# A chunked recurrence whose key products take all 128 rows of the array, with zeros where the solved values will stand, and one late gate instead of two

## The chip, the cores and the metric

The kernel runs on one core of one Trainium2 chip. The metric is device time in microseconds (us), start to end of one execution. The engines are named as in the profile: PE (TensorE, matrix products; PEld is its weight load), DVE (VectorE), ACT (ScalarE), POOL (GpSimd) and SP, whose queue issues nearly all transfers. Each engine takes its instructions in the order in which the program holds them; a semaphore holds an instruction back until what it reads is there.

## What is computed

One layer of a decoder trunk in float32: 512 tokens, width 1024. A combined projection feeds a dilated attention, a recurrent mixer (RWKV-7) of 16 heads and two gates; their gated sum goes through an output product, then a gated feed-forward part follows. The change lies in the recurrent mixer:

```python
def step(state, inp):
    r_t, w_t, k_t, v_t, aa_t, bb_t = inp
    sa = jnp.einsum('bhvk,bhk->bhv', state, aa_t)
    state = state * w_t[:, :, None, :] + sa[..., None] * bb_t[:, :, None, :] + v_t[..., None] * k_t[:, :, None, :]
    return state, jnp.einsum('bhvk,bhk->bhv', state, r_t)
...
_, y = lax.scan(step, state0, (tm(r_h), tm(w_h), tm(k_h), tm(v_h), tm(-kk), tm(kk * a_h)))
...
g_att, g_rwkv = jnp.split(jax.nn.sigmoid(gate_in + b_gate[l]), N_BRANCHES, axis=-1)
x = x + gt1 * ((g_att * y_att + g_rwkv * y_rwkv) @ w_o[l])
```

Every `sa` depends on the state after the token before, so the heads' recurrences are sequential in the tokens.

## The kernel before

Exact products of float32 matrices are made of three products each, of a rounded high part and the rest (`whi`, `wlo`, `hhi`, `hlo`): eight blocks of the contraction make 24 products of 128x128 by 128x512 on PE for one block of 128 output columns. Such a block is called a body.

**The recurrence** goes through the 512 tokens in 8 chunks of 64. The 16 heads form four groups of four; a group consists of two pairs `i` = 0, 1 of two heads `h` each. For a group, `pair()` makes r, k, v, decays and the Gram matrices `gt` of the chunks (on PE with the names `pg`, `pt`, `pn`); `inverse()`, and `inverse16()` for the last group, invert the triangular part of all chunks on DVE, with a few small products at the end (`pe`); `chain()` then runs the chunks one behind the other. A chunk `c` consists of:

- `state` (planned as `xy`): into the accumulator `xy` go the products of the carried state with the row matrix (`xy<-mbd,ar`, from the second chunk on) and the products of the Gram matrix with the values (`xy<-uv,gt`); these last are the keys' products of the title;
- `state_out`: the products of the carried state for the output, `xo<-mbd,ar`;
- `xs` on ACT copies `xy` out, `solve` multiplies it by the inverse (`u<-xs,gt`), and `solved` on ACT writes the result into `uv`;
- `update` (`u<-uv,bkt`) and `carry` on DVE make the new state `mbd`; `mp` on POOL multiplies the old state by its decay beforehand;
- `outs` (`xo<-uv,gt`) adds the output's share of the chunk; `norm` scales the outputs by two chunks.

The tile `uv` holds, for two chunks at once, values and solved quantities side by side: of its 128 rows, 64 hold the values of a chunk and the other 64 are what `solved` fills; which half is which changes with the chunk and with `i` (`R[i]`, `X[i]`). `values` (`u<-cen,v`) and `value` on ACT fill the first half for both chunks. There are two buffers of it. The keys' product reads the 64 rows of values alone, `outs` reads all 128.

**The order** is made when the program is built. `Plan` simulates the engines with a cost for each task that is written beside it, with priorities and with counted buffers; the sequence in which its tasks start becomes each engine's order. The keys' product is line 1804; the planned costs of `state` and `state_out` are in lines 1850 and 1851. Tasks of the recurrence have the first priority; bodies of projections, gates and later products have the last on PE and take what is left, in the order of their numbers.

**The gates** are 16 bodies (`pg`). An early gate is computed before its consumers' buffers exist, stored to memory (`gate_d`) and loaded again. The attention output's products (`pa`) need the attention halves `a`, which `att_parts` loads (`raw<-att_d`), casts on ACT and subtracts on DVE (line 2052). That may start only when all work that uses an earlier memory pool is done, all early gates among it. A late gate (`self.late`, line 1079) is computed after that point, straight into its place. The last products are `pr`, the recurrent mixer's output weights.

The weights come through two buffers, `raw`, of 1024 elements per partition; they are shared with the attention halves' load.

Of the kernel before, what the change touches and what calls it, by code (L numbers as in the profile page):

```python
# [10 lines left out]
F32 = mybir.dt.float32  # L11
# [7 lines left out]
P = 128  # L19
S = 512  # L20
D = 1024
KD = D // P
# [95 lines left out]
C_, E_, W_, V_, I_, M_, S_, U_ = 0.0, 1.0, 2.0, 200.0, 200.15, 220.0, 1.0, 10.0  # L118
# [10 lines left out]
class Layer:  # L129
# [911 lines left out]
    def rwkv(self, tail):  # L1041

        nc, tc, pl = self.nc, self.tc, self.pl
        self.cw, self.cps, self.ip, self.pps = [Late() for _ in range(4)]
        self.gps = [Late(), Late()]
        es, pre, even = self.rw_ctx, self.pre_ctx, ExitStack()

        def open_():
            self.att_ctx.close()
            pool = lambda st, room, name, bufs=1, **kw: setattr(  # L1050
                room, "pool", st.enter_context(tc.tile_pool(name=name, bufs=bufs, reuse_waits="tile", **kw)))
            pool(es, self.cw, "cw", 2)
            pool(es, self.gps[1], "gp1", 4)
            pool(es, self.cps, "cps", space=PSUM)
            pool(es, self.ip, "ip")
            pool(even, self.gps[0], "gp0", 4)
            pool(pre, self.pps, "pps", space=PSUM)

        def half():

            nc.vector.tensor_reduce(self.half, self.ident.rearrange("p (q s y) -> p s q y", q=4, s=2), axis=AX.XY,
                                    op=ALU.add)

            self.eye = self.ip.tile([P, 16], F32, name="eye")
            nc.vector.tensor_reduce(self.eye, self.ident.rearrange("p (q s y) -> p s y q", q=4, s=2)[:, 1], axis=AX.X,
                                    op=ALU.add)
        self.opened = pl.add("NO", 0, open_, list(pl.tasks), name="open")
        self.y_d = self.dr.tile([P, KD, S], F32, name="y_d")
        self.halved = pl.add("DVE", 0.3, half, [self.opened], M_)
        self.prs = [[{}, {}] for _ in range(4)]  # L1070
        self.grp = [{} for _ in range(4)]
        self.gd, self.gdt = {}, {}
        self.lora()
        for g in range(4):
            for i in range(2):
                self.pair(g, i)
            (self.inverse16 if g in (3,) else self.inverse)(g)
            self.chain(g)
        self.late = range(6, KD)
        for m in range(2 * KD):  # L1080
            if m not in self.late:
                self.early_gate(m)

        def close_pre():
            pre.close()
            self.more = tail()

        def close_even():
            even.close()
            self.more()  # L1090

        t0 = pl.add("NO", 0, close_pre, [t for t in pl.tasks if "pre" in t.marks])
        t1 = pl.add("NO", 0, close_even, [t0, self.grp[0]["all"][0], self.grp[2]["all"][0]])
        self.gates(t0)
        self.att_out(t0)
        self.rwkv_ahead(t1)
        T = mybir.EngineType
        with tc.manual_schedule(engines={T.PE, T.DVE, T.Activation, T.Pool, T.SP}):
            pl.run()
# [645 lines left out]
    def chain(self, g):  # L1745

        nc, pl, cw = self.nc, self.pl, self.cw
# [4 lines left out]
        d, uvs, yts = {}, {}, {}  # L1752

        T_ = 150.0 if g < 3 else 0.03
        pe = lambda us, fn, deps, prio=C_, **kw: pl.add("PE", us, fn, deps, prio, **kw)
        sca = lambda us, fn, deps, prio=C_, **kw: pl.add("ACT", us, fn, deps, prio, **kw)
# [7 lines left out]
        def values(c):  # L1764

            for n, i, x in ((0, 0, 0), (0, 1, 0), (1, 1, 1), (1, 0, 1)):
                r = 64 * (i ^ x)
                self.mm(d["u"][r : r + 64, n * P : n * P + P], prs[i]["v"][:, (c + x) * C : (c + x + 1) * C], self.cen,
                        n == 0, n == 1)

        def value(c, x):
            if x == 0:
                uvs[c] = cw.tile([P, 2, 256], F32, tag="uv", name=self.n("uv"), bufs=2)
            b = uvs[c].rearrange("p x (i n) -> p (x i) n", i=2)[64 * x : 64 * x + 64]
            nc.scalar.copy((b[:, 1:3] if x else b[:, 0:4:3]), d["u"][64 * x : 64 * x + 64, :].rearrange("p (i n) -> p i n", i=2))

        t = dve(0.35, begin, [gr["inv"], prs[0]["vd"], prs[1]["vd"], self.prev_chain] if g else
                [gr["inv"], prs[0]["vd"], prs[1]["vd"]])
        start = pl.join([t] + [t for i in range(2) for t in prs[i]["all"]])
        mb, uvd, last_uv = [], {}, start  # L1780
        norms, all_, used = [], [], []

        def vals(c):
            t = pe(0.54, lambda: values(c), [start, last_uv])
            t = sca(0.38, lambda: value(c, 0), [t], C_, take=("uv",))
            uvd[c] = uvd[c + 1] = sca(0.38, lambda: value(c, 1), [t], C_)
        vals(0)
        for c in range(NCH):
            e, q, cp = c % 2, c // 4, (c % 4) // 2

            R = [slice(64 * (e ^ i), 64 * (e ^ i) + 64) for i in range(2)]
            X = R[::-1]
            gt = lambda i, h, rows, cols, e=e, q=q, cp=cp: prs[i]["gt"][rows, e ^ i, 4 * q + 2 * cp + h, cols]
            s = {}
# [3 lines left out]
            def state(c=c, s=s, gt=gt, R=R, X=X, ih=ih):  # L1798
                xy = s["xy"] = ps("xy")
                s["uv"] = uvs[c - c % 2][:, c % 2]  # L1800
                for i in range(2 if c else 0):
                    self.mm(xy[X[i], :P], prs[i]["ar"][:, c, X[i]], mbd(i), True, False)
                for i, h, cs, ci in ih:
                    self.mm(xy[X[i], cs], gt(i, h, R[i], X[i]), s["uv"][R[i], ci], c == 0 and h == 0, h == 1)

            def state_out(c=c, s=s, R=R):

# [39 lines left out]
                    yts[c // 2] = cw.tile([P, 2, P], F32, tag=f"yt{c // 2}", name=self.n("yt"), bufs=1)  # L1847
                nc.scalar.copy(yts[c // 2][:, c % 2, :], s["xo"][:, :P])

            st = pe(0.6 if c else 0.33, state, [uvd[c], start] + mb, take=("xy",), name=f"xy{g}.{c}")  # L1850
            so_ = pe(0.33 if c else 0.0, state_out, [st], C_ + 0.01, take=("xo",), name="xo")
            x = sca(0.29, xs, [st], take=("xs",), give=("xy",))
            mpt = pl.add("POOL", 1.06, mp, mb, C_, take=("mp",)) if 0 < c < NCH - 1 else None
            so = pe(0.33, solve, [x, last_uv], give=("xs",), name="u")
# [3 lines left out]
            if c < NCH - 1:  # L1858
                up = pe(0.5, update, [last_uv], name="w")
                mb = [dve(0.36, lambda i=i, carry=carry: carry(i), [up, mpt, so_], give=("mp",) if mpt and i else ())  # L1860
                      for i in range(2)]
# [16 lines left out]
        for i in range(2):  # L1878
# [40 lines left out]
            t = pl.add("DMA", 0.6, g2_load, [start], W_, take=("g2",), lag=2.0)  # L1919
            t = sca(0.6, g2_hi, [t], T_)  # L1920
            t = dve(0.6, g2_lo, [t], T_)
            t = pe(1.05, gate, [t, self.sgs], S_, take=("t", "gg"), give=("g2",), name="gg")
# [21 lines left out]
        for i, (yl, gt_, gated, m) in enumerate(after):  # L1944
            t = dve(0.75, gated, [*ts[i], gt_], T_, give=("gg",))
            if g < 2:
                t = pl.add("DMA", 0.8, lambda i=i, m=m: nc.sync.dma_start(self.y_d[:, m, :], ys[i]), [t], M_,
                           give=("y",), lag=2.0)
# [456 lines left out]
```

## Time and profile before

| | us |
|---|---|
| three runs | 1211.57, 1217.01, 1217.90 (median 1217.01) |
| the profiled execution, its own time | 1212.94 |
| its span, from the first instruction to the last | 1211.2 |
| granted TensorE clock over the span | 0.993 of full speed |
| first keys' product of the first recurrence, last one of the last | 445.6, 743.2 |

Busy shares come as tenths in 40 equal slices of 30.3 us each (9 is 90% or more):

```profile
PE   4999998999999999999999999999999999999997
DVE  5688862431668986855797564764566665652235
POOL 4000000000000103122102222003000000000001
```

The recurrences lie in slices 15 to 25. In the prediction's rows of the timeline the columns are start, length, engine, line, operation, `out<-in` by the program's names, shape and count; in square brackets stands idle time of the engine ahead of it and what ended it. A product of two float32 matrices shows as two records. Products overlap in the array, so the length of a row is longer than the time until the next one can start. For PE the shape begins with the part of the array that is used, rows*columns.

### The profile page before, as it was taken

The page shows a single profiled execution, that of the slowest core. Times are in us where ns is not written, and L with a number is a line of the kernel's source. Part 1 is how long each engine was busy: PE and PEld are TensorE (multiplying, and loading weights), DVE is VectorE, ACT ScalarE, POOL GpSimd, SP SyncE. Part 2 cuts the span into 40 slices and gives each one's busy share as a digit, 9 for nine tenths or more (in the row PEclk, how much of TensorE's full clock was granted, in tenths as well). Part 3 has the DMA queues.
Part 4 walks back from the last instruction along what each step waited for, and adds up shares of the span by engine and source line. Part 5 has one row for each costly group of instructions (what it writes and reads, how often), then busy time and mean ns, then how long its engine had stood idle before and what let it go on. Part 6 is the DMA issues. An engine that isn't in the chain of part 4 may idle for free.

```text
span 1211.2 us, 18982 instructions
## 1 busy us (share of the span) xinstructions
PE 1170.6 (97%) x7456; PEld 945.9 (78%) x7456; DVE 737.5 (61%) x1248; ACT 542.3 (45%) x1014; POOL 108.6 (9%) x228
## 2 busy tenths in 40 slices
PE   4999998999999999999999999999999999999997
PEld 3788887889777776767787667788888888888886
DVE  5688862431668986855797564764566665652235
ACT  4475521622565555364636453444444444441223
POOL 4000000000000103122102222003000000000001
PEclk9999999999999999999999999999999999999999
DMA  9845871130143342422332335460233333332331
GB/s 316 257 131 171 280 223 56 53 91 18 23 135 95 83 115 78 122 74 75 87 97 86 117 94 159 155 209 18 70 97 94 104 88 105 89 117 93 103 122 70
DMA packets 168040, 138.39 MB, mean 114 GB/s; under 512 B 8753, under 2 KB 150155, under 8 KB 167951
## 3 DMA queue, kind: packets, MB, share of 16 engines
q1 hardware_dynamic: 167807, 136.93, 37.2%
q8 instruction: 58, 0.95, 0.3%
q14 instruction: 31, 0.25, 0.1%
q10 hardware_dynamic: 144, 0.26, 0.1%
HBM read 127.13 MB, written 10.04 MB: 113 GB/s over the span
## 4 chain that ended last, share of the span: by engine, by line
PE 81%; DVE 8%; DMA 6%; ACT 2%; issue 2%; SPq 0%; POOL 0%; POOLq 0%; DVEq 0%; ACTq 0%
PE u L148 22%; PE o L148 13%; PE v L148 7%; PE pg L148 7%; PE qk L148 6%; PE r L148 3%; DMA araw<-in_w_ada_dram 3%; PE k L148 3%; PE pa L148 2%; PE early L148 2%; PE po L148 2%; PE xy L148 2%; PE pr L148 2%; PE xo L148 2%; PE pt L151 1%
## 5 line engine op out<-in xcount | busy, mean ns | idle before, releaser
L194 DVE TENSOR_TENSOR wlo<-raw,whi 128x1024 fp32r<-128x1024 f32 x65 | 79.6, 1225 | 141.1 <-ACT whi L193 141.1
L148 PE MATMUL u<-h2hi,whi 128*128 128x512 f32 (+2 forms) x368 | 140.6, 382 | 0.0
L148 PE MATMUL u<-h2lo,whi 128*128 128x512 f32 (+2 forms) x368 | 140.6, 382 | 0.0
L148 PE MATMUL u<-h2hi,wlo 128*128 128x512 f32 (+2 forms) x368 | 140.5, 382 | 0.0
L1141 ACT CAST whi<-raw 128x1024 fp32r<-128x1024 f32 (+2 forms) x73 | 72.6, 994 | 119.6 <-PE qk L148 45.5
L193 ACT CAST whi<-raw 128x1024 fp32r<-128x1024 f32 x65 | 68.5, 1054 | 97.3 <-PE o L148 53.7
L1144 DVE TENSOR_TENSOR wlo<-raw,whi 128x1024 fp32r<-128x1024 f32 (+2 forms) x73 | 83.7, 1148 | 19.5 <-ACT whi L1141 19.3
L148 PEld LDWEIGHTS u<-h2hi,wlo 128*128 128x128 f32 x368 | 69.1, 188 | 13.2
L148 PEld LDWEIGHTS u<-h2hi,whi 128*128 128x128 f32 x368 | 69.1, 188 | 13.2
L148 PEld LDWEIGHTS u<-h2lo,whi 128*128 128x128 f32 x368 | 69.1, 188 | 13.2 <-POOL h2lo L405 0.2
L2231 DVE SCALAR_TENSOR_TENSOR u<-u,cols,u 128x511 f32<-128x511 f32 x88 | 65.7, 746 | 4.5 <-ACT u L2229 3.0
L148 PE MATMUL qk<-hhi,wlo 128*128 128x512 f32 x160 | 64.0, 400 | 0.0
L148 PE MATMUL qk<-hhi,whi 128*128 128x512 f32 x160 | 63.6, 398 | 0.0
L148 PE MATMUL qk<-hlo,whi 128*128 128x512 f32 x160 | 63.6, 397 | 0.0
L148 PE MATMUL o<-whi,fhi 128*128 128x512 f32 x144 | 56.1, 390 | 0.3 <-DVE u L2231 0.3
L148 PE MATMUL o<-whi,flo 128*128 128x512 f32 x144 | 56.0, 389 | 0.0
L148 PE MATMUL o<-wlo,fhi 128*128 128x512 f32 x144 | 56.0, 389 | 0.0
L148 PE MATMUL pg<-hlo,whi 128*128 128x512 f32 x128 | 52.0, 406 | 0.0
L148 PE MATMUL pg<-hhi,whi 128*128 128x512 f32 x128 | 51.6, 403 | 0.0
L148 PE MATMUL pg<-hhi,wlo 128*128 128x512 f32 x128 | 51.5, 403 | 0.0
L810 DVE CUSTOM_DVE_ANT_0 sm<-sc,m 128x256 f32<-128x256 f32 (+1 forms) x64 | 23.9, 404 | 37.6 <-PE sc L148 36.5
L347 DVE SCALAR_TENSOR_TENSOR acc<-araw,cols,acc 128x1024 f32<-128x1024 f32 x28 | 35.9, 1281 | 17.3 <-DMA araw<-in_w_ada_dram 17.1
(450 smaller groups left out, 2761.3 us busy)
## 6 DMA issues: line engine op xcount, KB each, us to landing
raw<-in_w_in_dram SPq DMA_DIRECT2D x62, 512.0 KB
raw<-in_w_up_dram SPq DMA_DIRECT2D x44, 512.0 KB
araw<-in_w_ada_dram SPq DMA_DIRECT2D x32, 512.0 KB
raw<-in_w_down_dram SPq DMA_DIRECT2D x22, 512.0 KB
araw<-in_w_ada_dram SPq DMA_DIRECT2D x32, 256.0 KB
wvraw<-in_w_in_dram SPq DMA_DIRECT2D x20, 256.0 KB
raw<-in_w_rwkv_out_dram SPq DMA_DIRECT2D x8, 512.0 KB
raw<-in_w_o_dram SPq DMA_DIRECT2D x8, 512.0 KB
```

The source lines that it names most:

```text
L148: return self.nc.tensor.matmul(out, lhsT, rhs, start=start, stop=stop)
L151: self.nc.tensor.matmul(out, in_, self.ident[: in_.shape[0], : in_.shape[0]], is_transpose=True, start=start, stop=stop,)
L193: self.nc.scalar.copy(hl[0], raw)
L194: (lo_eng or self.nc.vector).tensor_tensor(hl[1], raw, hl[0], op=ALU.subtract)
L347: nc.vector.scalar_tensor_tensor(d["acc"], raw, ck, d["acc"], op0=ALU.mult, op1=ALU.add)
L810: nc.vector.tensor_tensor_reduce(d["sm", h][:, :wd], d["sc"][h][:, :wd], m[:, 256 - wd : 256] if gi == 0 else m[:, :wd], 1.0, 3.0e38, op0= ...
L1141: nc.scalar.copy(d["w"][0], d["raw"])
L1144: nc.vector.tensor_tensor(d["w"][1], d["raw"], d["w"][0], op=ALU.subtract)
L2231: nc.vector.scalar_tensor_tensor(u[:, d:], pu[:, : S - d], ch(c), u[:, d:], op0=ALU.mult, op1=ALU.add)
```

## The change

From `chain()`'s value tasks on, the new file's line numbers are six higher (1810 for 1804).

```diff
-        self.late = range(6, KD)
+        self.late = range(7, KD)
...
+        def zero(c):
+
+            uvs[c] = cw.tile([P, 2, 256], F32, tag="uv", name=self.n("uv"), bufs=2)
+            for x in range(2):
+                b = uvs[c].rearrange("p x (i n) -> p (x i) n", i=2)[64 * x : 64 * x + 64]
+                nc.gpsimd.memset((b[:, 0:4:3] if x else b[:, 1:3]), 0.0)
+
         def value(c, x):
-            if x == 0:
-                uvs[c] = cw.tile([P, 2, 256], F32, tag="uv", name=self.n("uv"), bufs=2)
             b = uvs[c].rearrange("p x (i n) -> p (x i) n", i=2)[64 * x : 64 * x + 64]
...
             t = pe(0.54, lambda: values(c), [start, last_uv])
-            t = sca(0.38, lambda: value(c, 0), [t], C_, take=("uv",))
+            z = pl.add("POOL", 0.6, lambda: zero(c), [start], C_, take=("uv",))
+            t = sca(0.38, lambda: value(c, 0), [t, z], C_)
...
                 for i, h, cs, ci in ih:
-                    self.mm(xy[X[i], cs], gt(i, h, R[i], X[i]), s["uv"][R[i], ci], c == 0 and h == 0, h == 1)
+                    self.mm(xy[X[i], cs], gt(i, h, slice(0, P), X[i]), s["uv"][:, ci], c == 0 and h == 0, h == 1)
...
-            st = pe(0.6 if c else 0.33, state, [uvd[c], start] + mb, take=("xy",), name=f"xy{g}.{c}")
-            so_ = pe(0.33 if c else 0.0, state_out, [st], C_ + 0.01, take=("xo",), name="xo")
+            st = pe(0.5 if c else 0.33, state, [uvd[c], start] + mb, take=("xy",), name=f"xy{g}.{c}")
+            so_ = pe(0.24 if c else 0.0, state_out, [st], C_ + 0.01, take=("xo",), name="xo")
```

The keys' product reads all 128 rows of `gt` and of `uv`. So that the half which is not solved yet adds nothing, `zero` fills it beforehand, with two memsets on POOL for each pair of chunks. Two planned costs of PE tasks are smaller. Gate 6 becomes an early gate and is stored and loaded like the others; gate 7 alone is late.

Because the plan is made anew, the order moves in many places of the recurrences; three are shown. On PE, the seventh chunk of the third group (`xy`, `u`, `xo`), and the first small products of the last group's inverse (`pe`). Before:

```order
L148 MATMUL xo_6739<-uv_6709,gt_5237 64x64 x4
L148 MATMUL pe_6779<-lr_6428,gt_5842 32x16 x64
L148 MATMUL xy_6851<-mbd_84,ar_4969 64x128
L148 MATMUL xy_6851<-mbd_85,ar_5505 64x128
L148 MATMUL xy_6851<-uv_6709,gt_5237 64x64 x4
L148 MATMUL xo_6859<-mbd_84,ar_4969 64x128
L148 MATMUL xo_6859<-mbd_85,ar_5505 64x128
L148 MATMUL pe_6779<-lt_6429,lr_6428 32x16 x64
L148 MATMUL u_6223<-xs_6862,gt_5237 64x64 x4
L148 MATMUL pa_6722<-a_6510,whi_6661 128x512
```

The same place on PE now:

```order
L148 MATMUL xy_6729<-uv_6554,gt_5255 64x64 x4
L148 MATMUL xo_6743<-mbd_84,ar_4973 64x128
L148 MATMUL xo_6743<-mbd_85,ar_5502 64x128
L148 MATMUL pe_6747<-lr_6478,gt_5927 32x16 x64
L148 MATMUL u_6241<-xs_6812,gt_5255 64x64 x4
L148 MATMUL pe_6747<-lt_6479,lr_6478 32x16 x64
L148 MATMUL u_6241<-uv_6554,bkt_4975 64x64 x2
L148 MATMUL u_6241<-uv_6554,bkt_5504 64x64 x2
L148 MATMUL xo_6743<-uv_6554,gt_5255 64x64 x4
L148 MATMUL pa_6926<-a_6642,whi_6909 128x512
```

The two bursts `pe` moved ahead by a chunk, and the first `pa` of all now stands behind them; before, a whole body but two products of `pa` stood ahead of them.

On DVE, the attention halves' subtractions (`a<-raw,a`) and the steps of the last group's inverse (`lr`, `lt`). Before:

```order
L1656 TENSOR_TENSOR lr_6428<-lt_6429 128x72
L1658 TENSOR_REDUCE lt_6429<-lr_6428 128x6x2
L1659 SCALAR_TENSOR_TENSOR lt_6429<-lt_6429,sup_6533 128x6
L2052 TENSOR_TENSOR a_6507<-raw_6511,a_6503 128x512
L2052 TENSOR_TENSOR a_6508<-raw_6511,a_6504 128x512
L2052 TENSOR_TENSOR a_6509<-raw_6526,a_6505 128x512
```

The subtractions now, on DVE:

```order
L1677 STREAM_TRANSPOSE lr_6478<-lt_6479 128x512
L2058 TENSOR_TENSOR a_6646<-raw_6650,a_6642 128x512
L2058 TENSOR_TENSOR a_6647<-raw_6650,a_6643 128x512
L2058 TENSOR_TENSOR a_6648<-raw_6673,a_6644 128x512
L2058 TENSOR_TENSOR a_6649<-raw_6673,a_6645 128x512
L1976 TENSOR_REDUCE var_6829<-sq_6822 128x4
L1144 TENSOR_TENSOR wlo_6910<-raw_6824,whi_6909 128x512
```

They moved from among the inverse's steps to behind its transposition, which is what the first burst `pe` reads; `raw_6824`, the first weight of `pa`, takes the buffer of `raw_6650`.

On POOL, the second to fifth chunk of the first group: the decayed state (`mp`) and, before the change, what stood between:

```order
L1819 TENSOR_SCALAR mp_4176<-mbd_84,pc_3227 128x128
L1819 TENSOR_SCALAR mp_4176<-mbd_85,pc_3337 128x128
L1819 TENSOR_SCALAR mp_4268<-mbd_84,pc_3227 128x128
L1819 TENSOR_SCALAR mp_4268<-mbd_85,pc_3337 128x128
L1974 TENSOR_SCALAR var_4296<-var_4296 128x4
```

The same chunks on POOL now:

```order
L1825 TENSOR_SCALAR mp_4181<-mbd_84,pc_3227 128x128
L1825 TENSOR_SCALAR mp_4181<-mbd_85,pc_3337 128x128
L1776 MEMSET uv_4259 64x256
L1776 MEMSET uv_4259 64x2x128
L1825 TENSOR_SCALAR mp_4266<-mbd_84,pc_3227 128x128
L1825 TENSOR_SCALAR mp_4266<-mbd_85,pc_3337 128x128
```

The zeros of the third pair of chunks (the fifth and sixth chunk) stand ahead of the third chunk's `mp`.

## The prediction

> **What bounds the kernel now.** I read the page first (shares of the engines, chain that ended last), then a table of windows over the recurrence, then the timeline of TensorE in one chunk.
>
> ```profile
> span 1211.2 us, 18982 instructions
> PE 1170.6 (97%) x7456; PEld 945.9 (78%) x7456; DVE 737.5 (61%) x1248; ACT 542.3 (45%) x1014; POOL 108.6 (9%) x228
> PE 81%; DVE 8%; DMA 6%; ACT 2%; issue 2%; SPq 0%; POOL 0%; POOLq 0%; DVEq 0%; ACTq 0%
> ```
>
> ```profile
> 440.00:688.00 248.00, 247.12 (x2312) 183.31 (x2308) 180.20 (x356) 130.41 (x284) 49.37 (x90) 1.00 0.32 95
> 688.00:698.00 10.00, 7.32 (x228) 5.66 (x228) 1.98 (x3) 3.89 (x10) 0.25 (x1) 0.83 0.11 25
> 698.00:760.00 62.00, 61.75 (x572) 43.43 (x571) 33.70 (x64) 28.80 (x72) 15.21 (x27) 1.00 0.39 120
> 760.00:790.00 30.00, 27.63 (x113) 21.67 (x112) 23.66 (x30) 13.46 (x16) 0.00 (x0) 0.94 0.53 164
> ```
>
> The columns of the windows are length, then busy time of PE, PEld, DVE, ACT and POOL, then PEclk. The four recurrences run from 445 to 747. From 440 to 760 PE stands still 0.88 + 2.68 + 0.25 = 3.8 of 320 us: projections, gates and output products fill every wait of the recurrence. So in this stage the number of PE microseconds counts, not the latency of a chunk. What follows, to 788, is a chain of weight loads, two buffers deep. The chain of waits tells what starts it:
>
> ```profile
> 758.48 0.04 DVE gate L2122
> ...
> 760.22 1.23 DVE w L1984
> ...
> 761.46 4.88 DMA raw<-in_w_o_dram
> ...
> 781.34 4.18 DMA raw<-in_w_rwkv_out_dram
> ...
> 787.99 5.29 PE pr L148 x22
> ```
>
> Its first link is the gate product at 758.48, which waits for PE's first finished output block. It therefore moves with PE, and so does all after it.
>
> **The change on PE.** One chunk of the last recurrence, from the timeline (start, length; the first shape is the array tile, rows*columns):
>
> ```profile
> 720.52 0.44 PE L148 MATMUL xy<-mbd,ar 128*64 128x128 f32 x4
> 720.89 0.45 PE L148 MATMUL xy<-uv,gt 64*64 64x64 f32 x8
> 721.27 0.44 PE L148 MATMUL xo<-mbd,ar 128*64 128x128 f32 x4
> 721.64 0.50 PE L148 MATMUL pa<-a,whi 128*128 128x512 f32 x1
> ...
> 724.03 0.45 PE L148 MATMUL u<-uv,bkt 128*64 128x64 f32 x8
> 724.31 0.61 PE L148 MATMUL u<-cen,v 128*64 128x128 f32 x8
> 724.75 0.40 PE L148 MATMUL xo<-uv,gt 128*64 128x64 f32 x8
> 725.08 0.50 PE L148 MATMUL pa<-a,wlo 128*128 128x512 f32 x1
> ...
> 746.64 0.45 PE L148 MATMUL xo<-uv,gt 128*64 128x64 f32 x8
> 747.02 0.50 PE L148 MATMUL pr<-ylo,whi 128*128 128x512 f32 x1
> ```
>
> Only the distance between starts is time on PE. Eight records of 64 columns in 128*64 tiles take 0.28 when the shape changes ahead of them alone (724.03), 0.33 when it changes behind them alone (724.75), 0.38 with both (746.64): so 0.05 to enter, 0.10 to leave, 0.15 for a change of shape, and 0.23 bare. The product of the keys today, 64*64 with both changes, takes 721.27 - 720.89 = 0.38, bare 0.23 too: with all 128 rows it costs no more. The eight records of 128 columns at 724.31 have no change on either side: 0.44, so the four of `xy<-mbd` are 0.22 bare and 0.37 now, as the trace has them.
>
> Now: 0.37 + 0.38 + 0.37 = 1.12. With one shape throughout: 0.05 + 0.22 + 0.23 + 0.22 + 0.10 = 0.82. A chunk gives **0.30 us** where the three stand together, 0.15 where filler stands between.
>
> ```profile
> L148 PE MATMUL xy<-uv,gt x256: 218/218/267, 445.6 to 743.3; 64*64 64x64 f32 x128
> L148 PE MATMUL xy<-mbd,ar x112: 272/298/323, 451.1 to 742.8; 128*64 128x128 f32 x112
> ```
>
> 256 records are 32 chunks, 112 are the 28 that have a carried state; the four first chunks stay as they are between products of full shape. In the new order 26 of the 28 stand together: 26 x 0.30 + 2 x 0.15 = 8.1. Counting changes of shape on PE from the first chunk through the output products, the old order has 277 and the new one 220, and 57 x 0.15 = 8.5. I take **-8.3 us**.
>
> A rule of the Trainium skill speaks against it: TensorEngine Tiling (Array Packing), section Tiling Modes, has four independent tiles of 64*64 and only two of 128*64. By that rule the four products of a chunk could lose side-by-side running; by this sum they lose nothing. The 0.23 of both shapes above decides against it, and the loss is kept as a rival.
>
> **The zeros on POOL.** 16 pairs of chunks get two memsets each, 64 x 256 elements.
>
> ```profile
> L1641 POOL MEMSET lt<- 128x256 f32 x1 | 0.3, 313 | 0.0
> ```
> ```profile
> 725.74 0.72 POOL L1819 TENSOR_SCALAR mp<-mbd,pc 128x128 f32<-128x128 f32 x2 [5.45 <-DVE mbd L1837]
> ```
> ```profile
> 725.04 0.61 DVE L1837 SCALAR_TENSOR_TENSOR mbd<-u,pc,mp 128x128 f32<-128x128 f32 x2 [1.34 <-PE u L148]
> ...
> 730.30 0.61 DVE L1837 SCALAR_TENSOR_TENSOR mbd<-u,pc,mp 128x128 f32<-128x128 f32 x2
> ```
>
> Two of 0.313 are 0.63 a pair, 10 us of POOL in all, and POOL was busy 9%. In the order each later pair's zeros stand about two chunks ahead of the copy that needs them, two times the 5.26 us between the carries above. `mp` is queued behind them; it ends at 726.46 and is wanted at 730.30, so 3.8 us cover 0.63. At the start of a recurrence the zeros run beside the values' product (0.44 at 724.31) and could show by 0.2 us, four times. I take 0, with 0 to +0.8 for the range; without any cover it would be +10.
>
> **The gate that moves.** Its 24 products stay on PE; its store and its load are two more issues on SP's queue, whose results are not wanted for tens of microseconds: 0. But the attention halves, which wait until the last early gate has closed its buffers, come one gate later, and now stand behind the last group's inverse on DVE. That touches the one place where PE stalled:
>
> ```profile
> 686.31 1.26 PE L148 MATMUL pe<-lr,gt 32*32 32x16 f32 x128
> 687.50 0.44 PE L148 MATMUL xy<-mbd,ar 128*64 128x128 f32 x4
> ...
> 689.17 1.26 PE L148 MATMUL pe<-lt,lr 32*32 32x16 f32 x128 [0.48 <-issue]
> 692.62 0.45 PE L148 MATMUL u<-xs,gt 64*64 64x64 f32 x8 [2.19 <-issue]
> ```
> ```profile
> 694.00:696.00 2.00, 2.00 (x18) 1.13 (x18) 0.69 (x1) 1.97 (x4) 0.00 (x0) 0.50 0.00 0
> ```
> ```profile
> 672.08 0.38 SPq L178 DMA_DIRECT2D raw<-in_w_att_out_dram  x1
> ```
> ```profile
> 675.03 0.62 ACT L1141 CAST whi<-raw 128x512 fp32r<-128x512 f32 x1 [0.58 <-DMA raw<-in_w_att_out_dram]
> ```
> ```profile
> 670.76 1.89 DVE L2052 TENSOR_TENSOR a<-raw,a 128x512 fp32r<-128x512 f32 x3
> ```
>
> Today 0.48 + 2.19 = 2.7 us are lost idle, with no releaser named, behind two bursts of narrow products; then PEclk is 0.50, and by 0.83 over the ten microseconds of the window above 0.17 x 10 = 1.7 more are lost. Together 4.4. In the new order the first `pa` needs a weight whose buffer two of the attention subtractions (2 x 0.63) must free: 1.26, then 2.95 from issue to cast (672.08 to 675.03) and 0.62 for the cast, 4.8 us after the transposition that also starts the bursts. PE has two bursts (2 x 1.19), a solve (0.38), an update (0.28) and `xo` (0.33) in front: 3.4. So PE must wait 1.4 us or more there. That wait and the unnamed one lie over each other. Ends: -3.0 (1.4 idle, clock kept) and +3.0 (4.0 idle and two stretches at half clock, 4.0 + 3.4 = 7.4). The nearest row is the stall itself, so I keep most of it: **-0.7**.
>
> The Trainium skill, TensorE: Matmul & The Clock Gate, section Part 1, has the clock halved after an idle window of about 3.4 us; here it fell after 2.7 idle, so the page's figure is not the limit. By the page a wait of 1.4 to 2.7 would keep the clock and the term would be -1.7 or better.
>
> **Sum.** -8.3 - 0.7 = -9.0. The profiled execution took 1212.94 (span 1211.2 and 1.7 around it), so 1203.9 for such a one. The three runs of before stand at -1.4, +4.1 and +5.0 from it; for the middle run after I add half of the 4.1: **1206**. Other moves in the order may open or close a microsecond of idle.
>
> **The rivals.**
> - *A deeper stall* (0.22). The weights of `pa` come one by one, the wait repeats, and the clock halves twice: +3.0 in place of -0.7, and 0.8 for zeros that show, -8.3 + 3.0 + 0.8 = -4.5, 1210 by the same reckoning. For it: the loads start only behind the subtractions. Against: later buffers come free while PE works on the first block.
> - *The change of shape is not what costs* (0.05), but the change of operand or of accumulator; then only the -0.7 is left, 1214. Against: 724.03 to 725.08 passes through two accumulators and three operand pairs without the 0.15.
> - *Products that share all rows wait for one another* (0.03): 0.23 more for each of 32 chunks, +7.4 - 8.3 - 0.7 = -1.6, 1213. Against: the bare 0.23 of both shapes. The rule on tiling modes above, of the Trainium skill, would give this case.
> - *Slower* (0.05): the zeros wait for the pair before, and `mp`, queued behind them, holds the carry, the next state and PE, which takes its queue in order. It decides once zeros and `mp` end more than the 3.8 us late; for +6 in the end 12 later pairs must lose (6 + 9) / 12 = 1.3 us each, so 5.1 us late every time, 1221. Nothing in the rows comes near it.
>
> **Chances.** About 0.5% (6.1 us) is what a measurement of this kernel can tell from no change. The forecast, -6.5 to -12, has 0.65. Faster by over 0.5%: 0.65. Within 0.5%: the deeper stall, the two cases without a gain, 0.30. Slower: 0.05. The range goes from -8.5 - 3.0 - 1 = -12.5 on the profiled execution, 1200, to -3.3 (8.1 gained, 3.0 + 0.8 + 1 lost) on the middle run, 1213.
>
> **What would show it.** In the new trace `xy<-uv` must read 128*64, `xy<-mbd` to the end of `xo<-mbd` must take 0.82, and PE must be as full from 440 to 760 with the first block's gate some 9 us before 758.48. The zeros must end before the value copies, `mp` well before its carry. It is wrong if the three runs together still take over 1.0, or if PE idle around the last inverse grows over 3 us.

## The result, and the profile after

The changed kernel takes **1206.09 us** (median of 6 runs, 1204.25 to 1208.97); the kernel before, on the same chip, 1216.7 (6 runs). The ratio of their times is 0.9919, 95% interval 0.9893 to 0.9945: 9.9 us faster by the ratio (the medians lie 10.6 apart). A second comparison on another occasion gave 0.9928 (0.9909 to 0.9947), 8.7 us. The profiled execution took 1206.07, its span is 1204.3 where it was 1211.2: 6.9 less. Two slow executions, one of the kernel before (1899.59) and one of rows_undone (6441.32), are left out of every figure below.

From the page of the changed kernel, then its windows over the recurrence (length; busy time of PE, PEld, DVE, ACT, POOL; PEclk), and the groups of the keys' product:

```profile
span 1204.3 us, 19054 instructions
PE 1165.9 (97%) x7456; PEld 948.3 (79%) x7456; DVE 738.7 (61%) x1248; ACT 542.0 (45%) x1014; POOL 114.5 (10%) x260
```
```profile
440.00:680.00 240.00, 238.16 (x2160) 180.04 (x2158) 175.61 (x346) 126.39 (x273) 50.07 (x109) 1.00 0.32 95
680.00:690.00 10.00, 8.09 (x313) 6.29 (x311) 5.60 (x11) 6.87 (x17) 3.63 (x7) 0.83 0.50 149
690.00:752.00 62.00, 62.00 (x653) 44.88 (x653) 35.65 (x66) 30.61 (x78) 17.06 (x33) 1.00 0.43 128
752.00:782.00 30.00, 29.31 (x128) 23.57 (x127) 22.59 (x28) 12.61 (x15) 0.00 (x0) 1.00 0.51 159
```
```profile
L148 PE MATMUL xy<-uv,gt x256: 219/222/311, 446.5 to 736.2; 128*64 128x64 f32 x128
```

The recurrence runs from 446.5 to 736.2: 289.7 where it was 743.3 - 445.6 = 297.7. Not all of these 8.0 us are the change of shape: 12 fewer products `pa` and `pr` of full size stand between its first and last keys' product, 12 x 0.23 = 2.8. PE is as full as before; the 30 us of the output products, 752 to 782 (760 to 790 before), lost 2.4 and now lose 0.7. A chunk with an odd number, on the timeline of PE:

```profile
674.77 0.44 PE L148 MATMUL xy<-mbd,ar 128*64 128x128 f32 x4
675.04 0.40 PE L148 MATMUL xy<-uv,gt 128*64 128x64 f32 x8
675.27 0.39 PE L148 MATMUL xo<-mbd,ar 128*64 128x128 f32 x4
675.59 0.50 PE L148 MATMUL pg<-hlo,whi 128*128 128x512 f32 x1
```

675.59 - 674.77 = 0.82, to the hundredth what was forecast. An even chunk, the first of its pair, is another matter. These are its rows on PE and those of DVE and ACT that belong to it; other rows in between are left out:

```profile
456.12 0.61 DVE L1843 SCALAR_TENSOR_TENSOR mbd<-u,pc,mp 128x128 f32<-128x128 f32 x2 [1.37 <-PE u L148]
456.81 0.76 ACT L1780 COPY uv<-u 64x256 f32<-64x256 f32 x2 [0.66 <-DVE mbd L1843]
457.25 0.44 PE L148 MATMUL xy<-mbd,ar 128*64 128x128 f32 x4
457.52 0.55 PE L148 MATMUL xy<-uv,gt 128*64 128x64 f32 x8
457.60 0.27 ACT L1854 COPY yt<-xo 128x128 f32<-128x128 f32 x1
457.92 0.44 PE L148 MATMUL xo<-mbd,ar 128*64 128x128 f32 x4
...
458.29 0.50 PE L148 MATMUL t<-sg0h,g2h 128*128 128x512 f32 x1
```

Here the three steps take 458.29 - 457.25 = 1.04. The copies of the pair's values on ACT start only when the carry on DVE has ended (456.73) and end at 457.57; the copy `yt<-xo`, which empties an accumulator, follows until 457.87. PE is at `xy<-uv` from 457.52 on, before the copies end, and it starts `xo<-mbd` at 457.92, 0.05 behind `yt<-xo`: 0.40 for products that are 0.23 bare. None of this carries an idle mark on PE, since the rows of products overlap by more than the wait.

The sum over all chunks (the distance from each record of the three steps to the next record, without idle time, half of it where the clock is 0.50) falls from 33.28 to 27.93: **-5.35**. (Both sums hold the keys' products of the four first chunks, 1.5; the expectations below call them sums over 28 chunks. At 0.82 in each of the 28 the sum would be 24.5.) Where the other time went, by the idle marks of PE: at the last inverse 2.68 before, 2.17 now, and one stretch of 3.41 at half clock in both; at the output products 2.37 and a stretch at half clock before, 0.69 and none now, -1.7 - 1.7 = **-3.4**; elsewhere 1.3 more idle, 0.7 of it ahead of the first product behind the blocks `o` (`tr`, at 804.96); and the recurrence begins 0.9 later, though nothing was changed ahead of it. There the stretches at half clock lasted 13.7 us in this execution and 6.8 in that of the kernel before.

The stall at the last inverse is still there, inside the second burst, and the first `pa` follows the chunk's update:

```profile
685.07 0.96 PE L148 MATMUL pe<-lt,lr 32*32 32x16 f32 x93 [1.25 <-issue]
...
686.71 1.22 PE L148 MATMUL pa<-a,whi 128*128 128x512 f32 x2
```

### The profile page after: what moved, and what is told of

Its sections match the earlier page's. It is cut to its first block, busy times and chain, and to the rows that moved or that the text cites. A ratio compares the mean times of both kernels' runs of the same rounds, so it can differ in the third digit from the quotient of the medians.

```text
span 1204.3 us, 19054 instructions
## 1 busy us (share of the span) xinstructions
PE 1165.9 (97%) x7456; PEld 948.3 (79%) x7456; DVE 738.7 (61%) x1248; ACT 542.0 (45%) x1014; POOL 114.5 (10%) x260
## 4 chain that ended last, share of the span: by engine, by line
PE 82%; DVE 8%; DMA 6%; ACT 2%; issue 2%; SPq 0%; POOL 0%; POOLq 0%; DVEq 0%; ACTq 0%
PE u L148 22%; PE o L148 11%; PE pg L148 8%; PE v L148 8%; PE qk L148 7%; PE r L148 3%; PE k L148 3%; PE pa L148 3%; DMA araw<-in_w_ada_dram 2%; PE early L148 2%; PE po L148 2%; PE xy L148 2%; PE pt L151 2%; PE sc L148 2%; PE xo L148 1%
## 5 line engine op out<-in xcount | busy, mean ns | idle before, releaser
L148 PEld LDWEIGHTS u<-h2hi,wlo 128*128 128x128 f32 x368 | 69.1, 188 | 13.2
L148 PEld LDWEIGHTS u<-h2hi,whi 128*128 128x128 f32 x368 | 69.1, 188 | 13.2
L148 PEld LDWEIGHTS u<-h2lo,whi 128*128 128x128 f32 x368 | 69.1, 188 | 13.2 <-POOL h2lo L405 0.2
L810 DVE CUSTOM_DVE_ANT_0 sm<-sc,m 128x256 f32<-128x256 f32 (+1 forms) x64 | 23.9, 404 | 37.9 <-PE sc L148 36.8
```

What stands on the lines that cost most here:

```text
L148: return self.nc.tensor.matmul(out, lhsT, rhs, start=start, stop=stop)
L810: nc.vector.tensor_tensor_reduce(d["sm", h][:, :wd], d["sc"][h][:, :wd], m[:, 256 - wd : 256] if gi == 0 else m[:, :wd], 1.0, 3.0e38, op0= ...
```

## The experiments

All were compared with the kernel before, run on the same occasion. On four occasions that kernel's "clock" lies at 13.1 to 13.9 and its "full" at 1198.8 to 1199.3; for the first comparison's runs of it no clock is on record. "Three steps" is the sum above. "Output" is PE's idle ahead of products `pr` and `o` between the last keys' product and the gated feed-forward part. "Inverse" is PE's idle at the last inverse, and behind the stroke the length of the stretch at half clock there, both in the profiled execution. "Clock" is the span times (1 - granted clock), mean over the runs, and "full" the median of span times granted clock: the time apart from the clock. The clock has three digits, so for one run both are good to about 0.6. "Full" is an estimate: it takes half of a stretch at half clock as lost. Among 86 runs of the kernel before the span grows by 0.75 us for each us of "clock", so "full" takes off somewhat too much where the clock's loss is large.

| kernel | median us (runs) | ratio, 95% interval | three steps | output | inverse | clock | full |
|---|---|---|---|---|---|---|---|
| before (34 runs of one comparison) | 1214.4 | | 33.3 | 2.4 | 2.7 / 3.4 | 13.2 | 1199.1 |
| changed | 1206.09 (6) | 0.9919 [0.9893, 0.9945] | 27.9 | 0.7 | 2.2 / 3.4 | 9.8 | 1194.6 |
| changed_again | 1204.66 (6) | 0.9928 [0.9909, 0.9947] | 28.3 | 0.7 | 2.2 / 6.8 | 9.6 | 1193.0 |
| keys_alone | 1212.64 (12) | 0.9987 [0.9972, 1.0002] | 27.5 | 5.8 | 2.0 / 10.2 | 13.8 | 1196.9 |
| gate_alone | 1211.90 (12) | 0.9987 [0.9966, 1.0008] | 33.9 | 0.0 | 0.9 / 17.1 | 14.5 | 1196.3 |
| rows_undone | 1211.62 (11) | 0.9979 [0.9967, 0.9992] | 34.2 | 0.7 | 2.1 / 3.4 | 11.1 | 1198.5 |
| copies_behind_carry | 1211.29 (12) | 0.9977 [0.9961, 0.9993] | 24.9 | 4.4 | 2.1 / 17.1 | 17.2 | 1191.6 |
| out_ahead | 1207.74 (12) | 0.9958 [0.9941, 0.9975] | 28.0 | 0.7 | 2.1 / 3.4 | 12.1 | 1194.6 |
| yt_ahead | 1205.47 (7) | 0.9933 [0.9910, 0.9956] | 27.5 | 0.7 | 2.8 / 3.4 | 11.2 | 1192.2 |
| both_ahead | 1202.59 (6) | 0.9914 [0.9888, 0.9940] | 26.2 | 0.7 | 2.9 / 3.4 | 9.8 | 1192.0 |
| both_again | 1202.38 (6) | 0.9909 [0.9883, 0.9936] | 26.2 | 0.7 | 2.6 / 3.4 | 8.6 | 1192.7 |
| bursts_split | 1215.43 (12) | 1.0014 [1.0000, 1.0028] | 33.3 | 5.2 | 0.0 / 0 | 11.3 | 1202.4 |
| no_late_gate | 1217.24 (12) | 1.0030 [1.0014, 1.0045] | 28.2 | 1.1 | 6.0 / 23.9 | 19.0 | 1196.5 |
| zeros_four | 1207.78 (6) | 0.9944 [0.9923, 0.9965] | 28.2 | 0.7 | 2.4 / 13.7 | 12.1 | 1193.1 |

### The two parts alone

keys_alone is the changed kernel with both late gates, gate_alone the kernel before with one. The order of each is made anew by its plan, so more differs than the part that is named.

```diff
-        self.late = range(7, KD)
+        self.late = range(6, KD)
```
```diff
-        self.late = range(6, KD)
+        self.late = range(7, KD)
```

> The changed kernel with two late gates (6 and 7) as before; the rest of the change stays. Theory: the change has two gains. The three steps of a chunk (xy<-mbd, xy<-uv, xo<-mbd) went from 33.3 us in 28 chunks to 27.9 (5.4), and that comes from the keys' products alone; the wait of PE for weights at 773 (1.60 + 0.53 idle and half clock behind it, together 3.8) shrank to 0.7 in the changed kernel because its first output block o stands further ahead on PE, and that comes from the gate. In this order the first o stands where it stood before. So here the three steps take 28 us, a wait of about 2 us with half clock stands again between 760 and 790, and the time is 5 us under before, a ratio of 0.9955. Rival, as the prediction had it: the gate itself is worth nothing, and this kernel is as fast as the changed one, 0.992.

> The kernel before with gate 7 alone late; keys' products on 64 rows, no zeros. Theory: the three steps stay at 33.3 us in 28 chunks, the first o stands further ahead as in the changed kernel, and PE waits under 1 us between 752 and 790 where it lost 3.8; the stall at the last inverse stays within 1 us of before's 4.4. Time 3 us under before, a ratio of 0.9975. Rival: the gate is worth nothing, 1.000; or the deeper stall, two stretches at half clock at the last inverse, +3, 1.0025.

The three steps came as expected, 27.5 and 33.9, but the times did not: neither part alone can be told from no change. The 0.9955 expected of keys_alone lies outside its interval. The kernel before waits at the output products for the weights' casts on ACT and DVE:

```profile
773.70 0.50 PE L148 MATMUL pr<-yhi,whi 128*128 128x512 f32 x1 [1.60 <-ACT whi L193]
...
774.96 0.62 PE L148 MATMUL pr<-yhi,wlo 128*128 128x512 f32 x1 [0.53 <-DVE wlo L194]
```

In keys_alone PE has 5.8 us less to do in the three steps, and it waits 5.8 there where it waited 2.4, so 3.4 of the 5.8 are given back:

```profile
754.76 0.74 PE L148 MATMUL pr<-yhi,whi 128*128 128x512 f32 x2 [1.30 <-ACT yhi L2083]
...
772.91 0.50 PE L148 MATMUL pr<-yhi,whi 128*128 128x512 f32 x1 [2.41 <-ACT whi L193]
```

In gate_alone this wait is gone (0.96 come back later, ahead of `tr`): the first output block `o` stands ahead of the last `pr` products, where it can fill it. The start of `o<-wohi,mhi` tells the place; in this order, the kernel before, the changed kernel, gate_alone and keys_alone:

```profile
L148 PE MATMUL o<-wohi,mhi x64: 387/389/482, 793.1 to 838.7; 128*128 128x512 f32 x64
```
```profile
L148 PE MATMUL o<-wohi,mhi x64: 387/389/497, 757.1 to 831.8; 128*128 128x512 f32 x64
```
```profile
L148 PE MATMUL o<-wohi,mhi x64: 387/389/482, 769.2 to 843.6; 128*128 128x512 f32 x64
```
```profile
L148 PE MATMUL o<-wohi,mhi x64: 387/389/482, 793.7 to 839.3; 128*128 128x512 f32 x64
```

Every kernel of the table in which `o` starts behind the `pr` products (before, keys_alone, copies_behind_carry, bursts_split) waits 2.4 to 5.8 us there, every one with `o` ahead 1.1 or less. copies_behind_carry has one late gate and `o` behind, and it waits 4.4, so it is the place and not the number of late gates that goes with the wait; no run moves `o` alone. Apart from the clock the kernels with one part are 2.2 and 2.8 faster than the kernel before, the changed kernel 4.5 to 5.8 in its two comparisons (the 4.5 against the runs before of another occasion). The rest of the gain lies in the clock, which the parts alone do not gain: 13.8 and 14.5, where the changed kernel has 9.8 and 9.6. In the profiled execution of gate_alone it is at half for 17 us. They begin in an idle piece inside a burst, and PE is hardly idle after it (the burst on the timeline, then the window).

```profile
689.39 1.36 PE L148 MATMUL pe<-lt,lr 32*32 32x16 f32 x86 [0.94 <-issue]
```
```profile
689.30:706.36 17.06, 16.96 (x284) 12.72 (x285) 5.98 (x11) 7.96 (x18) 2.67 (x5) 0.50 0.41 125
```

### The rows undone, with every place kept

```diff
-                    self.mm(xy[X[i], cs], gt(i, h, slice(0, P), X[i]), s["uv"][:, ci], c == 0 and h == 0, h == 1)
+                    self.mm(xy[X[i], cs], gt(i, h, R[i], X[i]), s["uv"][R[i], ci], c == 0 and h == 0, h == 1)
```

> The changed kernel with the keys' product back on the 64 rows of values; zeros, gate and every place in the order stay. Theory: changes of shape cost 0.15 each. In odd chunks the three steps go back from 0.82 to 1.12; in even chunks, where the changed kernel waits for the copies of the values and takes about 1.0 to 1.2, they come back to 1.12 to 1.2. Sum 16 x 0.30 + 0.6 = +5.4 on the changed kernel: a ratio of 0.9965 against before. Rival 1: the change of shape isn't what costs (it is the change of operand or accumulator): three steps stay at 0.82, ratio 0.992. Rival 2: all 57 changes of shape show, +8.3, ratio 0.9987.

The three steps are back at 34.2, 6.3 over the changed kernel, and the ratio at 0.9979. It lies between the two expectations; the interval holds the 0.9987 of the second rival and not the 0.9965. An even chunk of this kernel:

```profile
454.61 0.44 PE L148 MATMUL xy<-mbd,ar 128*64 128x128 f32 x4
454.98 0.45 PE L148 MATMUL xy<-uv,gt 64*64 64x64 f32 x8
455.35 0.44 PE L148 MATMUL xo<-mbd,ar 128*64 128x128 f32 x4
455.72 0.50 PE L148 MATMUL t<-sg0h,g2h 128*128 128x512 f32 x1
```

1.11, against 1.04 in the changed kernel for the same chunk. ACT's copies of the values end at 454.93 and `yt<-xo` at 455.22, 0.05 and 0.13 ahead of the products that need them: the changes of shape had been hiding the copies. So the change of shape is what costs, the first rival falls; and in even chunks its removal uncovers the copies.

This is the one run that takes back a part and leaves every place in the order. With the gate, the zeros and the order of the changed kernel, the shape is worth 0.0051 to 0.0060 of the time, 6.2 to 7.3 us, give or take 3 (3.9 to 5.5 apart from the clock); what is left of the change without it is worth 2.5 us, and 0.6 apart from the clock. keys_alone had shown 1.6 us for the shape, or 2.2 apart from the clock. So what a part is worth depends on the order around it, and the 2.2 and 2.8 are no shares of the gain.

### What holds the even chunks

Four edits of the changed kernel: the plan is told of the carry (which moves the order in many places); `xo<-mbd` ahead of the keys' product in even chunks; `yt<-xo` ahead of the values' copies on ACT; and these two together. The last three change 12 places on an engine and no other.

```diff
-            t = sca(0.38, lambda: value(c, 0), [t, z], C_)
+            t = sca(0.38, lambda: value(c, 0), [t, z] + mb, C_)
```
```diff
                 for i in range(2 if c else 0):
                     self.mm(xy[X[i], :P], prs[i]["ar"][:, c, X[i]], mbd(i), True, False)
+                if c and not e:
+                    s["out"](0)
                 for i, h, cs, ci in ih:
...
-            def state_out(c=c, s=s, R=R):
+            def state_out(late=1, c=c, s=s, R=R, e=e):
 
+                if late and c and not e:
+                    return
```
```diff
         def value(c, x):
+            if c and not x and d.get("xr") == c - 1:
+                d["out"]()
...
             def out(c=c, s=s):
+                if s.pop("done", 0):
+                    return
+                s["done"] = 1
```

> The changed kernel, whose plan is told that the copies of the values on ACT start behind the carry on DVE, as the trace has them (0.08 us behind it, 0.76 long). Theory: in the even chunks of the changed kernel PE reaches xy<-uv before the copies end and loses 0.17 to 0.41 us each, 2.9 in eleven chunks, which no idle time shows. With more filler ahead of them the three steps take 0.82 in even chunks too, 23 us in 28 chunks in place of 27.9. But the first o stands behind all pr products again in this order, so the 3.1 us of the wait for weights come back: time about that of the changed kernel, 0.992, made up differently. Rival: the even chunks are slow because products on all 128 rows of uv wait for one another, then the three steps stay at 1.0 to 1.2 there, and the ratio is 0.995.

> The changed kernel, with one exchange in the 12 even chunks that have a carried state: xo<-mbd stands ahead of xy<-uv; every other place in the order stays. Theory: in these chunks PE reaches xy<-uv before the copies of the values on ACT end and loses about 0.2 us, which no idle time shows; xo<-mbd, 0.22 bare, needs no copy and fills that wait. The three steps go from 27.9 us in 28 chunks to about 25.5; 2.2 us under the changed kernel, a ratio of 0.990 against before. Rival: the even chunks are slow because products on all 128 rows of uv wait for one another; then the 0.2 stay and the ratio stays 0.992.

copies_behind_carry, an even chunk (PE and ACT):

```profile
478.88 0.74 ACT L1780 COPY uv<-u 64x256 f32<-64x256 f32 x2
...
480.20 0.44 PE L148 MATMUL xy<-mbd,ar 128*64 128x128 f32 x4
480.47 0.40 PE L148 MATMUL xy<-uv,gt 128*64 128x64 f32 x8
480.70 0.39 PE L148 MATMUL xo<-mbd,ar 128*64 128x128 f32 x4
481.02 0.50 PE L148 MATMUL pg<-hhi,wlo 128*128 128x512 f32 x1
```

With the copies done before PE comes, 0.82: products that share all rows do not wait for one another. The three steps fall to 24.9, near the 24.5 that 0.82 everywhere would give. Apart from the clock the kernel is among the fastest, 1191.6, though its clock loss of 17.2 makes that figure look too good; it stood at half clock for 17 us at the inverse, and its `o` is behind, so the time is 1211.29, a ratio of 0.9977 where 0.992 was expected. out_ahead gained nothing (0.9958 beside the changed kernel's 0.9928 on the same occasion), and my reason for it was incomplete:

```profile
455.08 0.74 ACT L1780 COPY uv<-u 64x256 f32<-64x256 f32 x2 [0.66 <-DVE mbd L1849]
455.52 0.44 PE L148 MATMUL xy<-mbd,ar 128*64 128x128 f32 x4
455.85 0.27 ACT L1860 COPY yt<-xo 128x128 f32<-128x128 f32 x1
456.17 0.44 PE L148 MATMUL xo<-mbd,ar 128*64 128x128 f32 x4 [0.21 <-ACT yt L1860]
```

Now PE waits for `yt<-xo`, which ACT does behind the values' copies: the same row of copies, by its other end. Hence the exchange on ACT:

> The changed kernel, with one exchange on ACT ahead of each of the 12 even chunks that have a carried state: the copy of the last chunk's output (yt<-xo) stands ahead of the two copies of the values; every other place in the order stays. Theory: the lost time in even chunks is a row of three copies on ACT behind the carry on DVE, 0.08 + 0.76 + 0.27: the keys' product waits for the two copies of values, and xo<-mbd for the accumulator that the third one empties. That is why the exchange on PE won nothing: it only changed which copy PE waits for. With the third copy done earlier, ACT would sit idle there anyway, the even chunks still wait about 0.1 for the values, but xo<-mbd no longer waits: three steps 26.5 us in place of 27.9, 1.4 under the changed kernel, a ratio of 0.9915 where the changed one has 0.9925. Rival: products on all 128 rows of uv wait for one another, 27.9 and 0.9925.

> Both exchanges, on PE (xo<-mbd ahead of xy<-uv) and on ACT (yt<-xo ahead of the values' copies), on the changed kernel. Theory: now xo<-mbd finds its accumulator empty and fills the wait for the values; the three steps of even chunks take 0.82 to 0.87, 24.5 us in 28 chunks in place of 27.9; 3 us under the changed kernel at full clock, a ratio of 0.990 if the loss to the half clock stays at 10 us. Rival: 27.9 and 0.9925, as above.

both_ahead, the same chunk:

```profile
452.16 0.27 ACT L1866 COPY yt<-xo 128x128 f32<-128x128 f32 x1
452.64 0.76 ACT L1782 COPY uv<-u 64x256 f32<-64x256 f32 x2 [0.21 <-DVE mbd L1851]
453.13 0.44 PE L148 MATMUL xy<-mbd,ar 128*64 128x128 f32 x4
453.40 0.39 PE L148 MATMUL xo<-mbd,ar 128*64 128x128 f32 x4
453.62 0.40 PE L148 MATMUL xy<-uv,gt 128*64 128x64 f32 x8
453.95 0.50 PE L148 MATMUL t<-sg0h,g2h 128*128 128x512 f32 x1
```

453.95 - 453.13 = 0.82. The sum is 26.2, not the 24.5 expected. One even chunk still waits for the copies of the values (1.18, at 465.26). Two others (1.25 each, at 547.95 and 675.57) wait for the second half of the carry on DVE, which ends about 0.85 behind the first. And in the last two groups `xo<-mbd` stands apart from the other two steps in one chunk each. yt_ahead alone brought 0.4 to 0.8 instead of 1.4. The kernel of both exchanges has the lowest medians of all, 1202.59 and, repeated, 1202.38; its ratios of 0.9914 and 0.9909 lie below the changed kernel's 0.9919 and 0.9928, though the intervals overlap.

> The kernel of both exchanges once more, for a second interval beside the two of the changed kernel (0.992 and 0.993): theory 0.990 to 0.9915, the three steps again near the first run's sum and the two steps that the exchanges touch without a wait for a copy. Rival: the first run's 0.9914 was a good draw of the half clock; then 0.9925 or more.

### The stall at the last inverse

bursts_split is the kernel before with the two bursts cut in four pieces each, no_late_gate is out_ahead with gate 7 early too.

```diff
-            t = pl.add("PE", 2.6, lambda j=j: half_pe(j), [t, ey], 0.5, take=() if j else ("t",), name="pe")
+            for y in range(0, 16, 4):
+                t = pl.add("PE", 0.65, lambda j=j, y=y: half_pe(j, range(y, y + 4)), [t, ey], 0.5,
+                           take=() if j or y else ("t",), lag=0.5 if y < 12 else 0.0, name="pe")
```
```diff
-        self.late = range(7, KD)
+        self.late = range(8, KD)
```

> The kernel before, whose first two bursts of narrow products (pe, 128 records each) at the last inverse are split into four pieces each with other products between. Theory: the unnamed stall (0.48 + 2.19) stands there because PE works through a burst's instructions faster than they come, and the narrow products count little for the clock; split, the stall falls under 1 us and PE keeps its clock at this place, less about 1 us for six more changes of shape: 3 us under before, 0.9975. Rival: the stall has to do with the inverse (what the bursts read or write), then it stays at 2 us or more, and the ratio is 1.000 to 1.001.

> The kernel of out_ahead with gate 7 early as well, so that no gate is late. Theory: the first o stands ahead as in the changed kernel, so the wait for weights at 773 stays away; but no gate's products are left for PE at the last inverse until the first weight of pa is there, so the idle there grows from 2.2 to about 4 us and the clock halves for more than one stretch: 2 to 4 us slower than out_ahead, 0.992 to 0.993. Rival: one gate less beside the recurrence is once more worth 2 to 3 us, as it was from two to one: 0.988.

Split, the bursts leave no idle and no half clock at the inverse. The fillers between the pieces could cover any wait, so this alone does not tell what the stall is; its place does. Count PE's records in order of their starts, weight loads, products and semaphore instructions together. In all fourteen traces every idle mark `<-issue` of PE's products then stands at record 9409 or 9410, or at 9665 or 9666, which is 256 further on, whatever instruction is there. In most kernels it is a narrow product of the second burst; in the kernel before the 2.19 stand ahead of `u<-xs`, and in keys_alone 0.74 stand inside the keys' products:

```profile
685.61 0.39 PE L148 MATMUL xy<-uv,gt 128*64 128x64 f32 x7 [0.74 <-issue]
```

The 256 records ahead of 9409 went by in 1.3 to 2.6 us in the kernels, all thirteen others, that stall there, and in 4.5 us in bursts_split, which does not. So the stall belongs to a place in the stream of instructions that PE reaches early, not to what the products read or write. That the instructions come in pieces of 256 is a reading of this; no trace shows them coming.

But nothing was won: the last keys' product came at 748.6, 300.9 behind the first (297.7 before), with other products ahead of the pieces, and at the output products PE waited 5.2 where the kernel before waited 2.4, with two stretches at half clock:

```profile
760.47 0.78 PE L148 MATMUL pr<-yhi,whi 128*128 128x512 f32 x2 [2.01 <-ACT yhi L2079]
779.86 0.50 PE L148 MATMUL pr<-yhi,whi 128*128 128x512 f32 x1 [2.35 <-ACT whi L193]
```

no_late_gate is 9.5 us slower than out_ahead, where 2 to 4 were expected. Its first `pa` starts at 705.8 (686.3 in out_ahead), and until then PE has little to do:

```profile
688.06 1.37 PE L148 MATMUL pe<-lt,lr 32*32 32x16 f32 x88 [4.05 <-issue]
...
693.71 1.60 PE L148 MATMUL pe<-lr,gt 32*32 32x32 f32 x52 [1.26 <-issue]
```

That is the rival of the deeper stall, one gate further on: PE is at half clock for 23.9 us.

### The zeros, and the changed kernel again

```diff
-            for x in range(2):
+            for x in (0, 1) * 4:
```

> The changed kernel with the zeros written four times over, 2.5 us on POOL for a pair of chunks in place of 0.63. Theory: nothing waits for POOL within 2 us of it (mp, queued behind the zeros, then ends about 459.8 where its carry starts at 462.2), so the time stays, 0.9925, and mp ends before its carry in every chunk. Rival: the zeros cost what they take where they stand ahead of mp; 1.9 us more for 12 later pairs would show as up to 20 us, and with only a tenth of it 2 us, 0.994.

> The changed kernel as it is, beside the runs of this call. Theory: 0.992 against before, as in the first comparison; granted clock over the span 0.991 to 0.993, which is 9 to 10 us of loss to the half clock.

```profile
454.44 2.82 POOL L1776 MEMSET uv<- 64x256 f32 x8 [4.00 <-PE xo L148]
457.36 0.72 POOL L1825 TENSOR_SCALAR mp<-mbd,pc 128x128 f32<-128x128 f32 x2
```

Four times the zeros leave the time apart from the clock where changed_again has it (1193.1 and 1193.0), the three steps too (28.2 and 28.3); no carry waited for `mp`. The median is 3.1 higher than that of changed_again, with a longer stretch at half clock, 13.7 where the changed kernel had 3.4 and 6.8; that the zeros lengthen it is not shown. The ratio of 0.9944 alone could not tell 0.9925 from the rival's 0.994; the waits do.

## Why the prediction was right, and where it was not

The time, 1206, came out, and the mechanism of its largest term is shown. That the number is met to 0.1 us is luck: errors of both signs cancelled.

- **Shape, -8.3.** The price was right: 0.15 for a change, 0.23 bare for both shapes, 0.82 for a chunk. The order was right too: 26 of the 28 stand together. The size was not: 5.35. The step that failed is "26 x 0.30": it took each of them to run without a wait. In eleven of the twelve even chunks PE, now quicker, meets a row of three copies on ACT behind the carry, and the three steps take 0.99 to 1.30, 1.11 on average by the distances between the records. Eight of them are over 1.0, which the prediction had named as a sign of being wrong. In two of the eleven (552.49 and 679.79) PE waits for the second half of the carry, and DVE does that half behind ACT's copies. I had looked for a new wait on POOL, and not at ACT, where the copies had ended in the shadow of the changes of shape. The kernel before had a hint: in 13 places, 2.2 us in all, its view by tiles names ACT's copies (`ACT uv L1775`) as what ended the idle time of the weight loads of the keys' product.
- **Zeros, 0.** Right, with cover to spare.
- **The gate, 0 itself.** Not borne out by the profiles, where the output products give 3.4 us, which goes with the place of `o`. This is the step "What follows, to 788, is a chain of weight loads ... It therefore moves with PE, and so does all after it". It does not: keys_alone gave back 3.4 of its 5.8 us to that chain. The first block's gate came 4.5 us earlier (754.01 for 758.48), not the 9 that I named as a sign; the rest was won behind it. The three places of the order on which the prediction rests leave out a fourth, `o` among the `pr`. What this is worth in many runs is less clear: gate_alone is 2.8 faster apart from the clock, rows_undone with the same gate 0.6. Why the plans of some kernels put `o` ahead is open.
- **The stall, -0.7.** -0.5 in the profiled executions: 2.17 idle, and the same 3.41 at half clock. But of the 2.17 only 1.49 are the bursts' (0.24 for a copy on ACT and the unnamed 1.25); 0.68 are waits for the carry, which the prediction did not have. The expected wait for the first weight left no idle of its own: its cast ended at 686.34, and PE came to the first `pa` at 686.71, so the unnamed stall lay over it, as the prediction had it. The time at half clock differs from run to run, so its mean over many runs counts: 13.1 to 13.9 us of "clock" before (in four comparisons), 9.8 and 9.6 after. These 3 to 4 us are about a third of the timed gain. How much of them belongs to the last inverse is not shown: in the profiled executions stretches at half clock also stand near 37, 140 and 188 us, at 775 before, and at the end.
- **The sum, -9.0.** In the profiled executions -6.9: -5.4 - 3.4 - 0.5, with 2.4 lost again elsewhere. By the ratio of the runs -9.9. The profiled execution of the kernel before, from which the sum starts, was a quick one: 1211.2 us at 0.993 lose 8.5 to the clock, its runs 13.1 to 13.9 on average.
- **Rivals.** The change of shape is what costs (rows_undone). Products that share all rows do not wait (copies_behind_carry). The zeros are covered (zeros_four). The deeper stall exists: two or more stretches at half clock came at the last inverse in keys_alone, gate_alone, copies_behind_carry, no_late_gate and zeros_four, and in one of the two profiled executions of the changed kernel (6.8); idle of 4 us or more came in no_late_gate alone.

## What to carry to other kernels

When a step on the bounding engine gets shorter, list what each of its products waits for and when that ends, also where the trace shows no idle: what just fitted becomes the wait. A gain inside a stage is kept only if the next stage's loads or fillers move too, so try each part of a change alone before giving it the credit, and take it back once with every place of the final order kept: the two answers differed here, 1.6 and over 6 us, though each is good to 2 or 3 only. And where a clock can halve, compare times with and without it, over many runs.

## What the hardware showed that I had not expected

- The stretches at half clock at the last inverse last 3.41, 6.83, 10.24, 13.65, 17.07 or 23.89 us, all multiples of 3.41, and the same kernel had 3.41 in one execution and 6.83 in another. Within one execution their starts lie whole multiples of 3.413 us apart (before: 37.91, 188.10, 693.27 and 775.19, the last three 44, 192 and 216 such steps behind the first). The Trainium skill, TensorE: Matmul & The Clock Gate, section Part 1, has a window of 3.4 us that runs free of the kernel; the trace agrees. It ties the half clock to an idle window; here PE was idle for 0.94 us at one piece in gate_alone and then busy for 16.96 of 17.06 us at half clock, among bursts of 32*32 tiles.
- A wait of up to 0.4 us on PE can carry no idle mark, since the records of products are longer than the distance between them: an even chunk of the changed kernel took 1.23 in place of 0.82 without one.
- The idle time of PE for which the profile names nothing but `issue`, 0.19 to 4.05 us, stood at two places of its instruction stream in all these kernels, 256 records apart. Where PE took 4.5 us for the 256 records ahead of the first place (bursts_split) and not 1.3 to 2.6, there was none.
